# A two-layer encoder in one launch: 33 work slots instead of 30, a smaller ring for software DMAs, and the first MLP in stages of 6, 10 and 16 tiles

## The chip, the cores and the metric

The kernel runs on one core of a Trainium2 chip. Its time is the device time in microseconds (us), as a median of several runs; the profile is of one execution. Engines are TensorE (PE; its weight loads are PEld), VectorE (DVE), ScalarE (ACT), GpSimd (POOL) and SyncE (SP), which issues most DMAs.

## The reference, cut to what matters

The input is 512 tokens of 1024 values. Two pre-norm residual layers follow each other. Layer 0 has two attention groups side by side, layer 1 has 2-D neighbourhood attention, and each layer ends in a squared-ReLU MLP with 4096 hidden values:

```
def sq_relu_mlp(h, w_up, w_down):
    u = jax.nn.relu(h @ w_up)
    return (u * u) @ w_down
...
h = h + sq_relu_mlp(rmsnorm(h, norm_ffn[layer]), ffn_w_up[layer], ffn_w_down[layer])
...
q, k, v = jnp.split(h @ w_qkv, 3, axis=-1)
```

The first two lines of code are the MLP, the third its place in a layer, the last the start of layer 1's attention. All is float32.

## The kernel before, in words

**Number format.** Every float32 operand of a matmul is split into a high part, rounded to fp32r by an ACT copy, and a low part, the rest, by a VectorE subtraction. A product is three matmuls: high x high, high x low, low x high. Residual and activations lie transposed: hT has eight tiles of 128 features x 512 tokens.

**Slots.** Most intermediate results live in NSLOT = 30 tiles of 128 x 1024 (4 KB per partition each). A free list hands them out first in, first out (`take`, `give`); a new user waits until the last reader of the slot's former content is done. Weights as loaded lie in four further buffers (`raw`), the split weights in three pairs (`whi`, `wlo`).

**Two ways to multiply.** `product` (L445) and `product8` (L491) are plain: a tile of 128 outputs and 128 inputs costs three matmuls of 512 columns (`mm3`, L572). The class `Seven` (L338) takes two tiles of inputs, two of outputs and both halves of the tokens as a 2 x 2 block problem and does it in seven products of half the columns instead of eight: 21 matmuls of 256 columns (L418 to L420). For that it needs sums of the weight blocks, made on GpSimd by `seven_chunk` (L326 to L328), sums of the activations, made by `sums` (L360 to L366), and an addition of the seven results in `run` (L426 to L430). The split activations of such a product take 7 half slots for each pair of input tiles (`split`, L387 and L388).

**The MLP** (`mlp`, L1476). `SIZES[0] = (6, 10, 14, 2)` cuts the 32 tiles of U, the hidden values, into stages:

1. Six tiles of U by plain products, then their part of the down projection, also plain, over 4 + 4 output tiles. Beside it the input of the up projection is prepared for `Seven`.
2. Thirteen runs of `Seven`, two tiles of U each. `stage` (L1407) mixes ten tiles that come out split (`pair_evac`) with those that are kept raw (`raw_evac`): 14, and 2 more at the end.
3. The ten split tiles go through `product8`: eight output tiles at once in all eight banks, one row of weights after the other. Beside its matmuls, `convert` (L1469) turns the 14 raw tiles, as seven pairs, into the sums and splits that `Seven` wants, on VectorE and ACT, a step at a time; the steps keep the order of the program. `bias_rows` (L1441) runs beside it too and sends DMAs for layer 1 through SP's queue.
4. `Seven` over the seven pairs (u7), four groups of two output tiles (L1539 to L1546); each group ends in an evacuation that adds 1024 columns to two tiles of hT (L1543). In the first group `beside` splits the two last raw tiles.
5. `plain_last` (L1486): those two tiles in two plain products of four output tiles, evacuated by L1505.

Layer 1's MLP (`SIZES[1]`, `last_mlp`) has the same stages 1 to 4 and an end of its own.

**Weights.** Every product announces its chunks with `plan`; `weights(i)` splits two chunks ahead (`AHEAD`) and loads five ahead (`LOAD`). A chunk for `Seven` takes a slot when more than `reserve` slots are free, else a `raw` buffer (L322). `reserve` is 3 in the up stages, NSLOT (so never a slot) during stage 3, and 1 in stage 4.

**The start of layer 1** (L1557 to L1571). X, eight slots, holds hT times the norm's gain, split (L579, L580). `valuesC(0)` (L1625) multiplies X with 256 columns of weights in two chunks of four feature tiles: 32 groups of three matmuls (L1639 to L1641), the first 16 over feature tiles 0 to 3, the other 16 over tiles 4 to 7. `projC(0)` follows. When the third group has been issued, the sums of squares of hT are asked for (`sumsq_acc`, L587 and L589); after the 24th, `rows_r1` makes the row norms from them (L594, L602).

**Order.** Outside the opening and layer 1's attention (`fixed_order`) the framework orders the instructions of each engine by dependence and its own estimates; operations marked `held` keep the program's order.

**Software DMAs.** DMAs issued by GpSimd: eight small ones at the start (L144 to L151) and 32 in layer 1's attention that copy halves of K and Q (L1591, L1611, L1612). GpSimd also normalises the attention's weights (L1683). Their descriptors lie in a ring at the start of SBUF; `dynamic_dma_scratch_size` is its size per partition, 16384 bytes if it is not given.

Of the kernel before, what the change touches and what calls it, by code (L numbers as in the profile page):

```python
# [20 lines left out]
FF = 4 * D  # L21
EPS = 1e-6
NEG = -1e30
NSLOT = 30
ROWS = 8
COLS = 64
C_ID, C_I1, C_I2, C_ROPE = 0, 128, 178, 182
# [8 lines left out]
def encoder_kernel(ctx: ExitStack, tc: tile.TileContext, ins, out, dbg=None):  # L36
    nc = tc.nc
# [10 lines left out]

    free = list(range(NSLOT))

# [67 lines left out]
    def keep(shape, dt, name):  # L118
        return big.tile(shape, dt, tag=name, name=name)
# [127 lines left out]
    def rows(w, k0, nk):  # L247
        return w[k0 * P : (k0 + nk) * P, :].rearrange("(k p) n -> p k n", p=P)
# [5 lines left out]
    def plan(*spec, make=None):  # L254
        asked.append((make or chunk, spec))
        return len(asked) - 1
# [188 lines left out]
    def product(w, k0, xk, cols, evac, banks=None, kstep=2, stride=None, eng=None, order=None, nk=None):  # L445

        nk = nk or len(xk)
        runs = []  # L450
        for c, m in cols:
            if runs and runs[-1][1] + runs[-1][2] == c:
                runs[-1][2] += m
            else:
                runs.append([sum(r[2] for r in runs), c, m])
        ncols = sum(m for _, m in cols)
        offs = [sum(m for _, m in cols[:j]) for j in range(len(cols))]
        ids = []
        for kk in range(0, nk, kstep):
            n = min(kstep, nk - kk)  # L460
            if len(runs) > 1 and stride:
                src = w[(k0 + kk) * P : (k0 + kk + n) * P, :].rearrange("(k p) (z m) -> p k z m", p=P, m=stride)
                parts = [(0, ncols, src[:, :, 0 : len(runs), runs[0][1] : runs[0][1] + runs[0][2]])]
            else:
                src = rows(w, k0[kk // 2] if isinstance(k0, list) else k0 + kk, n)
                parts = [(o, m, src[:, :, c : c + m]) for o, c, m in runs]
            ids.append(plan(parts, n, ncols, None, eng))

        def run():
            bk = (banks or group)(len(cols))  # L470

            def one(kk, k, j):
                hi, lo = weights(ids[kk // kstep])
                x, o, m = xk[kk + k], offs[j], cols[j][1]
                mm3(bk[j][0:m, :], hi[:, k, o : o + m], lo[:, k, o : o + m], x[:, 0, :], x[:, 1, :],
                    kk + k == 0, kk + k == nk - 1)

            for kk in range(0, nk, kstep):
                n = min(kstep, nk - kk)
                last = kk + kstep >= nk  # L480
                for a in range(len(cols) if last else n):
                    for b in range(n if last else len(cols)):
                        one(kk, *((b, order[a] if order else a) if last else (a, b)))
                        yield MM3
                    if last:
                        j = order[a] if order else a
                        evac(j, bk[j][0 : cols[j][1], :])

        return run()
# [46 lines left out]
    def tiles(c0, n):  # L536
        return [(c0 + o, min(P, n - o)) for o in range(0, n, P)]
# [34 lines left out]
    def mm3(o, wh, wl, xh, xl, first, last):  # L572
        PE.matmul(o, wh, xh, start=first, stop=False)  # L573
        PE.matmul(o, wh, xl, start=False, stop=False)  # L574
        PE.matmul(o, wl, xh, start=False, stop=last)  # L575
# [727 lines left out]

    SIZES = (6, 10, 14, 2), (6, 10, 12, 4)

    def first_product(l):

# [8 lines left out]
        rb = keep([P, S], F32, "rb")  # L1318
        state = dict(c=SIZES[l][0], ids=None, plain=False, split=iter(()), late=iter(()))
        x7 = Seven(KD)  # L1320
# [155 lines left out]
    def mlp(l, last=None):  # L1476

        stage, ahead, later = first_product(l)
        reserve[0] = 3
        w = ins["ffn_w_down"][l]
        up4, gens4 = [], []

        def plain_last(k0, V):  # L1486
            left = list(V)
            gens4.extend(product(w, k0, up4, tiles(512 * c, 512), lambda j, b, c=c: ev(4 * c + j, b), nk=2 * len(V))
                         for c in range(2))

            def beside(m, i):
                if m == 0 and i % 8 == 4 and left:
                    w_ = left.pop(0)
                    for z in range(2):
                        U4.append(Slot())
                        up4.append(U4[-1].pair())
                        split(w_.t[:, S * z : S * z + S], up4[-1])
                    w_.free()

            return beside  # L1500

        U4 = []

        def ev(m, b):
            return DVE.tensor_tensor(hT[:, m, :], hT[:, m, :], b, op=ALU.add)  # L1505

        U, _, _, (at_u, _), _ = stage(SIZES[l][0])
        up = [s_.pair() for s_ in U]
        gens = [product(w, at_u, up, tiles(512 * c, 512), lambda j, b, c=c: ev(4 * c + j, b)) for c in range(2)]
        ahead()  # L1510
        for c, gen in enumerate(gens):
            for i, _ in enumerate(gen):
                later(c, i)
        for s_ in U:
            s_.free()
        U, R, V, (at_u, at_r), late = stage(*SIZES[l][1:])
        first = [k + z for k in at_u for z in range(2)]
        gen = product8(w, first, U, ev)
        u7 = Seven(2 * len(R))
        ids = [u7.plan(w, 256 * m, at_r) for m in range(4)]  # L1520
        k0 = 32 - 2 * len(V)
        beside = (last or plain_last)(k0, V)
        bias = iter(()) if last else bias_rows()
        reserve[0] = NSLOT
        work, at = convert(u7, R), 0
        for i, _ in enumerate(gen):
            if i in (1, 4, 6):
                next(late, None)
            next(bias, None)

            at += 9 * len(R) + 2
            while at > 0:
                next(work, None)
                at -= 8 * len(U) - 2
        for x in (work, bias):
            for _ in x:
                pass
        reserve[0] = 1
        for m in range(4):  # L1539

            def evac(w_):
                h2 = hT[:, 2 * m : 2 * m + 2, :]
                DVE.tensor_tensor(h2, h2, w_.t.rearrange("p (z n) -> p z n", z=2), op=ALU.add)  # L1543

            for i, _ in enumerate(u7.run(ids[m], evac)):
                beside(m, i)  # L1546
        u7.free()
        for gen in gens4:
            for _ in gen:
                pass  # L1550
        for s_ in U4:
            s_.free()
# [72 lines left out]
    def valuesC(g, banks):  # L1625

        ids = [plan([(0, 256, rows(w_qkv, kk, 4)[:, :, 2 * D + 256 * g : 2 * D + 256 * g + 256])], 4, 256)
               for kk in (0, 4)]

        def run():  # L1630
            bk = banks()
            VC[g] = []

            def one(c, k, i):
                hi, lo = (w[:, k, :] for w in weights(ids[c]))
                o = bk[i // 2][:, 256 * (i % 2) : 256 * (i % 2) + 256]
                x = XP[4 * c + k][:, :, i * P : (i + 1) * P]
                first = c == 0 and k == 0 and i % 2 == 0
                PE.matmul(o, x[:, 0], hi, start=first, stop=False, skip_group_check=True)  # L1639
                PE.matmul(o, x[:, 0], lo, start=False, stop=False, skip_group_check=True)  # L1640
                PE.matmul(o, x[:, 1], hi, start=False, stop=c == 1 and k == 3, skip_group_check=True)  # L1641

            for k in range(4):
                for i in range(4):
                    one(0, k, i)
                    yield 0.355
            for i in range(4):
                for k in range(4):
                    one(1, k, i)
                    yield 0.355  # L1650
                if i % 2:
                    VC[g].append(Slot())
                    v = VC[g][-1].t.rearrange("p (i h e) -> p i h e", i=2, h=4)
                    for ii in range(2):
                        src = bk[i // 2][:, 256 * ii : 256 * ii + 256].rearrange("p (h e) -> p h e", h=4)
                        r = hold["r1"][:, i - 1 + ii : i + ii]
                        ACT.activation(v[:, ii, :, 0:64], src, AF.Copy, scale=r)
                        soon(lambda v=v, ii=ii, src=src, r=r: DVE.scalar_tensor_tensor(
                            v[:, ii, :, 64:128], src, r, f32(v[:, ii, :, 0:64]), op0=ALU.mult, op1=ALU.subtract))

        return run()


# [376 lines left out]
```

## Time and profile before

| What | us |
|---|---|
| median of 3 runs | 1159.39 (1158.99 to 1159.63) |
| span of the profiled execution | 1157.2 |
| TensorE busy | 1146.8 |
| VectorE busy | 903.0 |
| ACT busy | 652.1 |
| GpSimd busy | 577.5 |
| thirteen up runs of layer 0 | 321.7 to 450.0 |
| its product8 | 450.0 to 505.2 |
| its seven-product groups (u7) | 505.2 to 574.7 |
| its last plain pair | 574.7 to 585.8 |
| first values of layer 1 | 585.8 to 597.1 |

The span runs from the first to the last instruction of the profiled execution, for which no other time is given; the runs' times also hold what lies around it. In the lines below, a row of the stretches gives start:end and length, then for each engine its busy time and, in brackets, its instructions; then the granted share of TensorE's clock, the share of the DMA engines, and GB/s. A row of a group gives line, engine, operation, output<-inputs, shapes and count, then the busy time, the mean ns of one, the idle time before them and what ended it. A row of the timeline gives start, duration, engine, line and operation.

### The profile page before, as it was taken

How to read it: one execution, taken by the hardware profiler on the slowest of the kernel's cores; microseconds unless marked ns; L12 is line 12 of the kernel's file. 1: busy time of each engine (PE TensorE's matmuls, PEld its weight loads, DVE VectorE, ACT ScalarE, POOL GpSimd, SP SyncE). 2: the span in 40 equal slices, each digit the busy share in tenths (PEclk: the TensorE clock that was granted, in tenths of full speed). 3: DMA queues.
4: the chain of work that ended last, by engine and by line, in shares of the span. 5: the costliest groups of instructions: out<-in, count | busy, mean ns of one | idle time of the engine just before them, and what ended most of it. 6: DMA issues, size and time to landing. Idle time of an engine off the chain costs nothing.

```text
span 1157.2 us, 20288 instructions
## 1 busy us (share of the span) xinstructions
PE 1146.8 (99%) x7276; PEld 1021.1 (88%) x7276; DVE 903.0 (78%) x1542; ACT 652.1 (56%) x1115; POOL 577.5 (50%) x708
## 2 busy tenths in 40 slices
PE   9999999999999999999999999999999999999997
PEld 7787888888899999899988998988889999988996
DVE  7887988878978887877685666668987788778675
ACT  6676876755346667433454556555553666743345
POOL 4366252216798882379402232231379889316930
PEclk9999999999999999999999999999999999999999
DMA  8322415122432326523436664443333233432332
GB/s 241 100 74 70 101 51 142 55 67 98 126 93 74 92 83 202 185 92 117 125 98 164 150 174 128 117 109 117 100 120 108 79 89 92 136 102 80 98 106 73
DMA packets 112148, 128.05 MB, mean 111 GB/s; under 512 B 9411, under 2 KB 94576, under 8 KB 112048
## 3 DMA queue, kind: packets, MB, share of 16 engines
q1 hardware_dynamic: 109424, 120.09, 35.4%
q0 software_dynamic: 2304, 6.31, 2.3%
q8 instruction: 57, 0.93, 0.4%
q14 instruction: 43, 0.35, 0.1%
q10 hardware_dynamic: 320, 0.36, 0.1%
HBM read 104.32 MB, written 6.29 MB: 96 GB/s over the span
## 4 chain that ended last, share of the span: by engine, by line
PE 96%; DVE 2%; DMA 1%; issue 1%; ACT 0%; POOL 0%; DVEq 0%; POOLq 0%
PE mm L573 9%; PE mm L575 9%; PE mm L574 9%; PE mm L418 4%; PE mm L420 4%; PE mm L419 4%; PE s L1097 3%; PE t L418 3%; PE t L420 3%; PE t L419 3%; PE o L1085 3%; PE s L573 3%; PE s L574 3%; PE s L575 3%; PE s L418 2%; PE s L420 2%
## 5 line engine op out<-in xcount | busy, mean ns | idle before, releaser
L573 PE MATMUL mm<-a,whi 128*128 128x512 f32 x440 | 178.6, 407 | 0.2
L332 ACT ACTIVATE whi<-a 128x896 fp32r<-128x896 f32 x105 | 99.7, 951 | 132.5 <-POOL a L328 39.2
L574 PE MATMUL mm<-a,whi 128*128 128x512 f32 x440 | 173.5, 394 | 0.0
L575 PE MATMUL mm<-a,wlo 128*128 128x512 f32 x440 | 173.5, 395 | 0.0
L333 DVE TENSOR_TENSOR wlo<-a,whi 128x896 fp32r<-128x896 f32 x105 | 133.1, 1272 | 49.2 <-ACT whi L332 46.1
L223 DVE TENSOR_TENSOR wlo<-raw,whi 128x1024 fp32r<-128x1024 f32 (+4 forms) x113 | 131.1, 1164 | 39.0 <-ACT whi L233 38.4
L233 ACT ACTIVATE whi<-raw 128x1024 fp32r<-128x1024 f32 (+3 forms) x116 | 109.1, 942 | 68.4 <-PE s L574 24.0
L418 PE MATMUL mm<-a,whi 128*128 128x256 f32 x410 | 115.1, 281 | 0.0
L420 PE MATMUL mm<-a,wlo 128*128 128x256 f32 x410 | 114.7, 280 | 0.0
L419 PE MATMUL mm<-a,whi 128*128 128x256 f32 x410 | 114.7, 280 | 0.0
L328 POOL TENSOR_TENSOR a<-a 128x128 f32<-128x128 f32 x105 | 102.9, 980 | 8.2
L326 POOL TENSOR_TENSOR a<-a 128x128 f32<-128x128 f32 x105 | 75.8, 722 | 57.3 <-DMA a<-in_ffn_w_up_dram 37.1
L575 PEld LDWEIGHTS mm<-a,wlo 128*128 128x128 f32 x440 | 82.5, 188 | 18.9
L573 PEld LDWEIGHTS mm<-a,whi 128*128 128x128 f32 x440 | 82.7, 188 | 17.6 <-issue 0.6
L574 PEld LDWEIGHTS mm<-a,whi 128*128 128x128 f32 x440 | 82.9, 188 | 15.3 <-DVE a L930 0.2
L327 POOL TENSOR_TENSOR a<-a 128x256 f32<-128x256 f32 x105 | 90.6, 863 | 8.2
L333 DVE TENSOR_TENSOR wlo<-raw,whi 128x896 fp32r<-128x896 f32 x51 | 62.4, 1226 | 35.4 <-ACT whi L332 35.4
L1683 POOL TENSOR_SCALAR p<-p,ti 128x256 f32<-128x256 f32 x64 | 35.6, 567 | 104.7 <-DVE ti L1682 91.5
L1105 POOL TENSOR_SCALAR p<-p,ti 128x512 f32<-128x512 f32 x64 | 45.0, 705 | 85.7 <-DVE ti L1104 63.6
L418 PE MATMUL t<-a,whi 128*128 128x256 f32 x296 | 83.1, 281 | 0.0
L419 PE MATMUL t<-a,whi 128*128 128x256 f32 x296 | 82.8, 280 | 0.0
L420 PE MATMUL t<-a,wlo 128*128 128x256 f32 x296 | 82.8, 280 | 0.0
(427 smaller groups left out, 3492.9 us busy)
## 6 DMA issues: line engine op xcount, KB each, us to landing
a<-in_ffn_w_up_dram SPq DMA_DIRECT2D x78, 256.0 KB
raw<-in_ffn_w_down_dram SPq DMA_DIRECT2D x38, 512.0 KB
raw<-in_od_w_qkv_dram SPq DMA_DIRECT2D x64, 128.0 KB
a<-in_ffn_w_down_dram SPq DMA_DIRECT2D x27, 256.0 KB
raw<-in_ffn_w_up_dram SPq DMA_DIRECT2D x26, 256.0 KB
raw<-in_ffn_w_down_dram SPq DMA_DIRECT2D x25, 256.0 KB
raw<-in_ffn_w_up_dram SPq DMA_DIRECT2D x12, 512.0 KB
a<-a SPq DMA_DIRECT2D x18, 256.0 KB
```

The source lines that it names most:

```text
L223: z = lambda: (eng or DVE).tensor_tensor(to, src, f32(high), op=ALU.subtract)
L233: ACT.activation(hi[:, 0:m], raw[:, 0:m], AF.Copy)
L327: POOL.tensor_tensor(r[:, 4:6], r[:, 2:3].to_broadcast([P, 2, P]), r[:, 0:7:6], op=ALU.add)
L328: POOL.tensor_tensor(r[:, 7], r[:, 3], r[:, 5], op=ALU.subtract)
L332: ACT.activation(hi[:, 0:896], raw[:, 128:1024], AF.Copy)
L333: DVE.tensor_tensor(lo[:, 0:896], raw[:, 128:1024], f32(hi[:, 0:896]), op=ALU.subtract)
L418: PE.matmul(o, wh, x[:, 0], start=kp == 0 and n in (0, 1, 3, 5), stop=False, skip_group_check=True)
L419: PE.matmul(o, wh, x[:, 1], start=False, stop=False, skip_group_check=True)
L420: PE.matmul(o, wl, x[:, 0], start=False, stop=kp == self.np - 1, skip_group_check=True)
L573: PE.matmul(o, wh, xh, start=first, stop=False)
L574: PE.matmul(o, wh, xl, start=False, stop=False)
L575: PE.matmul(o, wl, xh, start=False, stop=last)
```

## The change

NSLOT goes from 30 to 33, and the ring for software DMAs from 16384 to 4096 bytes per partition; the difference is three slots of 4096 bytes. `SIZES[0]` becomes (6, 10, 16, 0): the two last tiles of U are kept raw like the 14 others and form an eighth pair of u7, `convert` has eight pairs, and `plain_last` has nothing to do. In `valuesC(0)`, the second 16 groups run feature tiles 4 and 5 over all four token blocks first, and then 6 and 7 block by block; the other values (`g` > 0) keep their order.

```diff
-NSLOT = 30
+NSLOT = 33
...
-    SIZES = (6, 10, 14, 2), (6, 10, 12, 4)
+    SIZES = (6, 10, 16, 0), (6, 10, 12, 4)
...
         def plain_last(k0, V):
             left = list(V)
+            if not V:
+                return lambda m, i: None
             gens4.extend(product(w, k0, up4, tiles(512 * c, 512), lambda j, b, c=c: ev(4 * c + j, b), nk=2 * len(V))
...
                 for i in range(4):
                     one(0, k, i)
                     yield 0.355
+            late = 2 if g == 0 else 0
+            for k in range(late):
+                for i in range(4):
+                    one(1, k, i)
+                    yield 0.355
             for i in range(4):
-                for k in range(4):
+                for k in range(late, 4):
                     one(1, k, i)
                     yield 0.355
...
-    nc = _bacc.Bacc("TRN2", target_bir_lowering=False, num_devices=1)
+    nc = _bacc.Bacc("TRN2", target_bir_lowering=False, num_devices=1, dynamic_dma_scratch_size=4096)
```

## The prediction

> **What bounds the kernel now.** I read the page's engine totals and the chain that ended last first, then the busy times of five stretches, then what TensorE waited for.
>
> ```profile
> span 1157.2 us, 20288 instructions
> ...
> PE 1146.8 (99%) x7276; PEld 1021.1 (88%) x7276; DVE 903.0 (78%) x1542; ACT 652.1 (56%) x1115; POOL 577.5 (50%) x708
> ...
> PE 96%; DVE 2%; DMA 1%; issue 1%; ACT 0%; POOL 0%; DVEq 0%; POOLq 0%
> ```
>
> TensorE is busy 1146.8 of 1157.2 us and the chain is TensorE for 96%. Whatever shortens the kernel must take matmuls away, or some of the 10.4 us in which TensorE has none.
>
> ```profile
> core 0: us, PE busy (x) PEld busy (x) DVE busy (x) ACT busy (x) POOL busy (x), PEclk, DMA share, GB/s
> 449.99:505.18 55.19, 55.19 (x243) 45.08 (x242) 46.62 (x70) 24.36 (x36) 17.84 (x23) 1.00 0.56 177
> 505.18:574.69 69.51, 69.51 (x589) 69.40 (x588) 48.50 (x48) 27.98 (x33) 53.02 (x62) 1.00 0.35 111
> 574.69:585.83 11.14, 11.14 (x51) 9.01 (x49) 10.70 (x16) 8.54 (x14) 0.00 (x0) 1.00 0.40 114
> 585.83:597.14 11.31, 11.31 (x98) 11.31 (x96) 11.13 (x16) 4.96 (x8) 0.00 (x0) 1.00 0.37 106
> 1149.60:1157.20 7.60, 0.04 (x1) 0.00 (x0) 2.62 (x8) 2.21 (x6) 0.00 (x0) 0.74 0.62 187
> ```
>
> The first four rows are consecutive stages of layer 0's down projection and the start of layer 1: the ten single rows of weights (product8), the seven-product pairs (x588), the last plain pair (48 matmuls), the first values of layer 1 (96). TensorE has no gap in any of them, at full clock. The last row is the end: 7.6 us without matmuls, which the change leaves alone.
>
> ```profile
> PE o L157 <- POOL zeros L130: 1.0, 1, 1.0
> PE t L602 <- DVE ti L190: 0.2, 1, 0.2
> PE t L594 <- DVE acc L630: 0.2, 1, 0.2
> PE t L594 <- DVE acc L589: 0.2, 1, 0.2
> PE t L602 <- DVE r L1566: 0.2, 1, 0.2
> ```
>
> So of the 10.4 us, 1.0 lie at the start and 7.6 at the end. About 1.8 us are left for waits in between, the shown ones among them. That is the most that any better ordering can win.
>
> **The change part by part.** *Matmuls.* Layer 0's last two U tiles leave the plain product and become an eighth seven-product pair. Which tiles the up stage makes, and in which order, stays the same: thirteen pairs, the last one kept raw in both. The plain stage goes: 2 products x 4 tiles x 2 rows x 3 = 48 matmuls of 512 columns, 11.14 us by its row (232 ns each). The eighth pair adds 4 groups x 7 products x 3 = 84 matmuls of 256 columns. The row of that stage gives 69.51/588 = 118.2 ns each, so 9.93 us. The difference is **-1.21 us**, all on the path, because TensorE is the path.
>
> By the Trainium skill, TensorE: Matmul & The Clock Gate, section Back-to-back issue gap, a stream of load-and-multiply pairs sustains about 131 ns at 512 columns and 81 at 128; that would price the 48 at 6.3 us and the 84 at 6.8 to 11.0, a loss of 0.5 to 4.7. The rows above have 232 and 118 ns in this stream, so the trace does not agree.
>
> *Loads and splits of the pairs' weights.* Away go two 512 KB chunks with an ACT copy and a VectorE subtraction each; four chunks of 256 KB come, each with three GpSimd sums.
>
> ```profile
> L328 POOL TENSOR_TENSOR a<-a 128x128 f32<-128x128 f32 x105 | 102.9, 980 | 8.2
> L326 POOL TENSOR_TENSOR a<-a 128x128 f32<-128x128 f32 x105 | 75.8, 722 | 57.3 <-DMA a<-in_ffn_w_up_dram 37.1
> L327 POOL TENSOR_TENSOR a<-a 128x256 f32<-128x256 f32 x105 | 90.6, 863 | 8.2
> ```
>
> A chunk costs GpSimd 0.98 + 0.72 + 0.86 = 2.57 us, and TensorE uses one in 21 x 118.2 = 2.48 us. GpSimd loses 0.09 us per chunk, 2.9 us over 32. It starts on them inside the previous stage (17.84 us of it there, seven chunks ahead), and 32 x 2.57 = 82 us fit into 69.5 + 9.9 + 17.8 = 97. I take 0; without that lead the cost is +2.9 us. The new spare slots let every such chunk have a slot instead of sharing the four raw buffers with other loads: nothing gained either, as TensorE has no gap to close there.
>
> *Converting the eighth pair* (its sums and splits on VectorE, during product8).
>
> ```profile
> L388 DVE TENSOR_TENSOR a<-a,a 128x512 fp32r<-128x512 f32 x14 | 10.7, 762 | 0.7 <-ACT a L387 0.5
> L388 DVE TENSOR_TENSOR a<-sc,a 128x512 fp32r<-128x512 f32 x7 | 5.3, 761 | 0.0
> L360 DVE TENSOR_TENSOR sc<-a 128x512 f32<-128x512 f32 x7 | 5.1, 722 | 0.0
> L388 DVE TENSOR_TENSOR a<-a,a 128x256 fp32r<-128x256 f32 x7 | 3.5, 493 | 0.0
> L392 DVE TENSOR_TENSOR a<-a 128x256 f32<-128x256 f32 x7 | 3.4, 485 | 0.2
> L363 DVE TENSOR_TENSOR a<-a,sc 128x256 f32<-128x256 f32 x7 | 3.4, 485 | 0.2
> ```
>
> Seven pairs now; one costs 2 x 0.762 + 0.761 + 0.722 + 0.493 + 2 x 0.485 = **4.47 us**. VectorE's idle time in this stage is 55.19 - 46.62 = 8.57 us, so it rises from 84% to 93%. What must not come late behind it stands in the next rows: VectorE's split of the tenth row and its first evacuation, and on TensorE the first readers of both.
>
> ```profile
> 493.68 1.45 DVE L223 TENSOR_TENSOR wlo<-raw,whi 128x1024 fp32r<-128x1024 f32 x1 [0.78 <-ACT whi L233]
> ...
> 500.24 0.67 DVE L1505 TENSOR_TENSOR hT<-hT,s 128x512 f32<-128x512 f32 x1
> ```
>
> ```profile
> 495.40 0.39 PE L575 MATMUL s<-p,wlo 128*128 128x512 f32 x1
> 505.18 0.28 PE L418 MATMUL s<-a,whi 128*128 128x256 f32 x1
> ```
>
> The split ends at 495.13 and is read at 495.40: 0.27 us to spare. The evacuation ends at 500.91 and its bank is wanted at 505.18: 4.27 us. If all added work goes into idle time nothing is late; if none does, the split is late by 4.47 - 0.27 = 4.2 us. I take **+0.1**, because the idle time is nearly twice the added work.
>
> *The joint with layer 1.* The plain stage was also a cover of 11.14 us between the last seven-product group and the values. Without it hT 6 and 7 are ready only behind that group's evacuation (L426 to L430, L1543).
>
> ```profile
> 574.54 0.68 DVE L427 TENSOR_TENSOR a<-a,mm 128x512 f32<-128x512 f32 x1
> ...
> 579.19 1.22 DVE L1543 TENSOR_TENSOR hT<-hT,a 128x1024 f32<-128x1024 f32 x1
> ...
> 582.45 0.75 DVE L580 SCALAR_TENSOR_TENSOR a<-hT,gT,a 128x512 fp32r<-128x512 f32 x1
> ```
>
> ```profile
> 578.11 0.72 ACT L579 ACTIVATE a<-hT,gT 128x512 fp32r<-128x512 f32 x1 [2.27 <-DVE hT L1505]
> ```
>
> The chain ends at 580.41, 5.7 us after the last matmul of the group at 574.69. Three L1505 additions of the plain product stand inside it (0.6 us apart each); they go, and 3.9 us are left. Then come two ACT halves (0.72 and some 0.62, as they pipeline) and the VectorE halves (0.75): X 6 is whole about 5.5 us and X 7 about 6.2 us after the group. The values take 11.31/32 = 0.353 us per group of three. In the old order X 6 is wanted after 16 + 2 groups, 6.4 us, and X 7 after 19, 6.7 us: on the edge. In the new order X 4 and 5 run for eight groups first, and X 6 is wanted at 24 groups, 8.5 us, X 7 at 8.8. The reordering buys 2 us of cover and no matmul. One edge remains: X takes eight slots, the free list holds five when the pairs' 28 are given back, and the fifth is the evacuation's own, free only after L1543. X 4 is then whole at about 3.9 + 0.7 + 0.8 = 5.4 us and is wanted at 5.7. Bounds: 0, and 1.2 us if one 128x1024 split lands in front. I take **+0.2**.
>
> *What gets earlier.* The squares of hT 0 to 5 no longer queue behind the plain product's additions (VectorE was busy 21.8 of 22.5 us in those two stretches), so the wait of L594 for acc should go.
>
> ```profile
> 597.84 0.39 PE L573 MATMUL mm<-a,whi 128*128 128x512 f32 x1
> 598.41 0.27 PE L594 MATMUL t<-ones,acc 128*128 128x1 f32 x1 [0.18 <-DVE acc L589]
> ```
>
> The next start comes 0.57 us after a matmul that takes 0.23: 0.34 us lost. I take **-0.3**. The wait of L602 for L1566 behind it is a chain of small operations that stays.
>
> *The smaller ring.* Only GpSimd's own DMAs use it.
>
> ```profile
> q0 software_dynamic: 2304, 6.31, 2.3%
> ...
> a<-a POOLq DMA_DIRECT2D x16, 256.0 KB, 3.7
> ```
>
> Each comes down in 3.7 us, in bursts of four per pair of heads. If the ring held one burst no longer, GpSimd would wait up to 3.7 us in eight places, 30 us, with the attention's normalisations queued behind; if it holds it, nothing changes, and nothing can be gained. I take 0: no wait for a ring shows on any of these now, and 2304 packets over 16 engines are 144 each for the whole run. By the Trainium skill, DMA: Bandwidth & Descriptors, section Terms, a descriptor has 16 bytes, so 4096 bytes would be 256 of them, an estimate by which the ring does not even wrap; no run here shows it.
>
> **Sum:** -1.21 + 0.1 + 0.2 - 0.3 = -1.2 us, against the profiled span 1157.2: 1156.0. The page gives no other time for that execution; the median of the runs is 1159.39, 2.2 us above the span, and I carry that over: **1158.2**. This is 0.10%, and about 0.2% (2.3 us) is what a measurement of this kernel can tell from no change.
>
> **The rivals.**
> - *More waits go (faster).* Other slots and another order around the joint also take the waits that stay in my sum. For it: they are short and hang on VectorE. Against: 1.8 us is all there is, 0.3 of it already counted. At most 1159.4 - 1.2 - 1.5 = 1156.7, or 1156.4 if the two small losses stay away too.
> - *The joint takes the gain back.* X 4 or X 6 late by 1 to 2 us: 1159 to 1160.4. For it: margins of 0.3 and 2 us. Against: VectorE loses 5.5 us of additions there.
> - *VectorE overflows in product8 (slower).* Place: the tenth row's split and the evacuations at 500 to 505 us. Price: 4.2 us at most, 1162.4. It ends slower than before once less than 3.0 of the 8.57 us of idle time can be filled, and slower by over 0.2% once less than 0.7 can. For it: a margin of 0.27 us, and ACT and VectorE alternate on the splits. Against: 5.5 us of that idle time are L223's waits for ACT, in which other splits can run.
> - *Small matmuls are not half price, or the change does nothing.* If a 256-column one cost what a 512-column one does, 84 x 232 ns - 11.1 = +8.4, 1167.8. If the ring's size frees no usable slot or binds, the time is 1159.4 or far above. The rows of 118 ns and of 144 packets speak against both.
>
> **How the numbers follow.** Forecast 0.52 (1157.4 to 1159.0), more waits go 0.20, the joint 0.12, VectorE 0.12, the last 0.04. The range 1156.6 to 1161.0 leaves out a quarter of the faster case, most of VectorE's upper part and the last. Faster by over 0.2% (under 1157.07): 0.16 of the faster rival and 0.03 of the forecast, 0.19. Slower (over 1161.71): 0.07 of VectorE's, 0.01 of the joint, 0.03 of the last, 0.11. Within: 0.70.
>
> **What would show it.** 672 seven-product matmuls in about 79.4 us, directly followed by L1639; no plain stage; the wait of L594 for acc gone; VectorE near 51 us in product8; L1683 on GpSimd with no new wait. Wrong would be: a wait of TensorE for L223 or L1505 around 495 to 510 us, a gap among the values at L1639 to L1641, GpSimd's sums (L328) named by ACT with TensorE behind it, or a change outside layer 0's end and layer 1's start, where only the slots differ and I count nothing.

## The result: slower by 0.45%, and the profile after

| | before | after |
|---|---|---|
| median of four runs each, same chip | 1159.34 us (1158.99 to 1159.63) | 1164.41 us (1164.29 to 1164.54) |
| ratio, 95% interval | | 1.0045 (1.003 to 1.0059) |
| span of the profiled execution | 1157.2 us | 1162.6 us |

The forecast was 1158.2 us, its range ended at 1161.0. The changed kernel is 5.1 us slower than before. (In after, lines from L1488 on stand 2 and from L1655 on 7 lines lower than in before: L1545 is before's L1543.)

The page's engine totals and the chain that ended last, of after:

```profile
span 1162.6 us, 20364 instructions
...
PE 1148.2 (99%) x7312; PEld 1023.3 (88%) x7312; DVE 911.4 (78%) x1541; ACT 655.7 (56%) x1119; POOL 585.8 (50%) x720
...
PE 89%; POOL 4%; DVE 3%; issue 1%; ACT 1%; DVEq 0%; POOLq 0%; ACTq 0%
```

TensorE's share of the chain fell from 96% to 89%, and GpSimd, which had 0%, now has 4% of it. TensorE's own 99% hardly shows this: the time in which it counts as idle grew from 10.4 to 14.4 us, and part of its waits counts as busy (80.33 us in u7 below, where e3, a run below without waits in u7, has 79.10 for the same matmuls). The stretches of layer 0's product8 and u7 in after, and of everything from there to layer 1's MLP:

```profile
core 0: us, PE busy (x) PEld busy (x) DVE busy (x) ACT busy (x) POOL busy (x), PEclk, DMA share, GB/s
451.40:506.72 55.32, 55.32 (x242) 45.04 (x241) 51.22 (x74) 25.57 (x38) 21.48 (x26) 1.00 0.54 171
506.72:590.11 83.39, 80.33 (x673) 79.41 (x672) 61.96 (x63) 37.98 (x48) 60.30 (x70) 1.00 0.32 98
590.11:885.39 295.28, 294.18 (x1658) 254.00 (x1657) 214.13 (x469) 152.75 (x320) 97.24 (x147) 1.00 0.48 136
```

Product8 is as forecast: VectorE 51.22 us busy, no wait of TensorE. The plain stage is gone. But the 672 seven-product matmuls, forecast at 79.4 us, took **83.39**. What TensorE waited for, longest first:

```profile
PE mm L420 <- DVE wlo L333: 1.9, 2, 1.3
PE o L157 <- POOL zeros L130: 1.0, 1, 1.0
PE s L420 <- DVE wlo L333: 0.7, 1, 0.7
PE o L1641 <- ACT a L579: 0.5, 1, 0.5
PE mm L418 <- ACT whi L332: 0.5, 1, 0.5
```

Three of the five are the splits (L332, L333) of the pairs' weights, a wait that before didn't have at all. The wait of L1641 belongs to the joint with layer 1 and comes up again at the end. Two rows of the timeline of GpSimd, in the beginning of u7, show where it starts; the bracket is the idle time ahead of an instruction and what ended it:

```profile
509.73 0.46 POOL L328 TENSOR_TENSOR a<-a 128x128 f32<-128x128 f32 x1
520.92 0.63 POOL L326 TENSOR_TENSOR a<-a 128x128 f32<-128x128 f32 x1 [10.73 <-DMA a<-in_ffn_w_down_dram]
```

GpSimd stands still for 10.73 us and then works to the end with one more pause of 1.0 us. The stretch from there to its last sum:

```profile
520.92:583.15 62.23, 60.27 (x508) 59.76 (x507) 46.68 (x46) 26.66 (x34) 57.72 (x66) 1.00 0.28 86
```

66 sums are 22 chunks, 62.23 / 22 = **2.83 us** each, where TensorE uses one in 2.48. Ten chunks were done before the pause. In the timelines, the sums of the tenth end 18.8 us ahead of its first matmul, those of the eleventh, the first after the pause, 8.5 us, and those of the 22nd 3.6 us. So the lead goes down by a pause at once and then, beside the second pause, by some 0.35 us a chunk. At the 23rd TensorE waits for the first time, and there the order of the chunks counts too. Two rows of GpSimd and one of ACT:

```profile
557.87 0.46 POOL L328 TENSOR_TENSOR a<-a 128x128 f32<-128x128 f32 x1
...
559.64 0.46 POOL L328 TENSOR_TENSOR a<-a 128x128 f32<-128x128 f32 x1
```
```profile
560.14 1.79 ACT L332 ACTIVATE whi<-a 128x896 fp32r<-128x896 f32 x2 [4.17 <-POOL a L328]
```

The sums of GpSimd's 23rd chunk were done at 558.33, yet ACT stood idle until those of its 24th were done at 560.10, and then copied two chunks at once: GpSimd did these two in the other order than TensorE uses them. The same happens in the last group at 583.16. There, too, a split at 579.80 started 1.2 us after its copy was done, as VectorE was with work for layer 1 (L589, L580). Before has the same change of order at 534.20 (ACT idle for 3.25 us) and no wait of TensorE, so it is the short lead that makes such delays count. How much of u7's loss is theirs was not taken apart.

By stages of the spans, from the stretches of each kernel (us):

| | start | 13 up runs | product8 | u7 + plain pair | values to layer 1's MLP | that MLP | end |
|---|---|---|---|---|---|---|---|
| before | 321.70 | 128.29 | 55.19 | 80.65 | 294.35 | 269.19 | 7.8 |
| after | 322.62 | 128.78 | 55.32 | 83.39 | 295.28 | 268.80 | 8.4 |
| slots and ring alone (e1) | 322.81 | 128.45 | 55.33 | 80.33 | 294.59 | 269.69 | 8.6 |
| ring alone (e2) | 322.19 | 128.29 | 55.15 | 80.63 | 294.34 | 269.20 | 7.8 |
| reserve 3 (e3) | 322.71 | 128.48 | 55.30 | 79.10 | 294.83 | 268.73 | 8.4 |
| reserve 3, old order (f2) | 322.52 | 128.78 | 55.30 | 79.09 | 294.68 | 268.39 | 7.8 |
| reserve 3, slots local (g1) | 321.72 | 128.29 | 55.14 | 79.18 | 294.23 | 269.08 | 7.8 |

Of the 5.4 us between the spans of before and after, u7 has 2.7, and the rest is small shares in the start, the up runs, the values and the end.

### The profile page after: what moved, and what is told of

Its sections match the earlier page's. It is cut to its first block, busy times and chain, and to the rows that moved or that the text cites. A ratio compares the mean times of both kernels' runs of the same rounds, so it can differ in the third digit from the quotient of the medians.

```text
span 1162.6 us, 20364 instructions
## 1 busy us (share of the span) xinstructions
PE 1148.2 (99%) x7312; PEld 1023.3 (88%) x7312; DVE 911.4 (78%) x1541; ACT 655.7 (56%) x1119; POOL 585.8 (50%) x720
## 4 chain that ended last, share of the span: by engine, by line
PE 89%; POOL 4%; DVE 3%; issue 1%; ACT 1%; DVEq 0%; POOLq 0%; ACTq 0%
PE mm L573 9%; PE mm L575 8%; PE mm L574 8%; PE mm L420 3%; PE mm L419 3%; PE mm L418 3%; PE s L1097 3%; PE t L420 3%; PE t L419 3%; PE t L418 3%; PE o L1085 3%; PE s L574 2%; PE s L573 2%; PE s L575 2%; PE t L1072 2%; PE s L420 2%
## 5 line engine op out<-in xcount | busy, mean ns | idle before, releaser
L333 DVE TENSOR_TENSOR wlo<-a,whi 128x896 fp32r<-128x896 f32 x148 | 187.4, 1272 | 78.4 <-ACT whi L332 78.0
L332 ACT ACTIVATE whi<-a 128x896 fp32r<-128x896 f32 x148 | 140.2, 950 | 157.8 <-PE o L419 39.7
L573 PE MATMUL mm<-a,whi 128*128 128x512 f32 x434 | 176.3, 407 | 0.2
L326 POOL TENSOR_TENSOR a<-a 128x128 f32<-128x128 f32 x148 | 105.3, 711 | 137.5 <-DMA a<-in_ffn_w_up_dram 76.6
L574 PE MATMUL mm<-a,whi 128*128 128x512 f32 x434 | 171.2, 394 | 0.0
L223 DVE TENSOR_TENSOR wlo<-raw,whi 128x1024 fp32r<-128x1024 f32 (+4 forms) x111 | 130.5, 1180 | 34.7 <-ACT whi L233 34.1
L327 POOL TENSOR_TENSOR a<-a 128x256 f32<-128x256 f32 x148 | 140.0, 946 | 11.5
L233 ACT ACTIVATE whi<-raw 128x1024 fp32r<-128x1024 f32 (+3 forms) x114 | 106.7, 939 | 69.1 <-PE s L574 27.4
L328 POOL TENSOR_TENSOR a<-a 128x128 f32<-128x128 f32 x148 | 130.1, 879 | 11.6
L420 PE MATMUL mm<-a,wlo 128*128 128x256 f32 x420 | 117.9, 281 | 1.9 <-DVE wlo L333 1.9
L418 PE MATMUL mm<-a,whi 128*128 128x256 f32 x420 | 117.8, 281 | 0.5 <-ACT whi L332 0.5
L419 PE MATMUL mm<-a,whi 128*128 128x256 f32 x420 | 117.5, 280 | 0.0
L575 PEld LDWEIGHTS mm<-a,wlo 128*128 128x128 f32 x434 | 81.4, 188 | 18.6
L418 PE MATMUL t<-a,whi 128*128 128x256 f32 x304 | 85.2, 280 | 0.0
L419 PE MATMUL t<-a,whi 128*128 128x256 f32 x304 | 85.1, 280 | 0.0
L420 PEld LDWEIGHTS mm<-a,wlo 128*128 128x128 f32 x420 | 79.0, 188 | 2.4 <-DVE wlo L333 2.3
```

The source lines that it names most:

```text
L223: z = lambda: (eng or DVE).tensor_tensor(to, src, f32(high), op=ALU.subtract)
L233: ACT.activation(hi[:, 0:m], raw[:, 0:m], AF.Copy)
L327: POOL.tensor_tensor(r[:, 4:6], r[:, 2:3].to_broadcast([P, 2, P]), r[:, 0:7:6], op=ALU.add)
L328: POOL.tensor_tensor(r[:, 7], r[:, 3], r[:, 5], op=ALU.subtract)
L332: ACT.activation(hi[:, 0:896], raw[:, 128:1024], AF.Copy)
L333: DVE.tensor_tensor(lo[:, 0:896], raw[:, 128:1024], f32(hi[:, 0:896]), op=ALU.subtract)
```

## The experiments

Three theories were set against each other for u7 and for the rest; the expectations call them A, B and D. **A:** layer 1's first loads, which in SP's queue stand ahead of the pairs' loads, bring those late. **B:** the number of buffers that chunks can lie in caps how far GpSimd gets ahead, and as it is slower than TensorE it never makes that good. **D:** the three slots shift the work of other stages too. Medians stand beside those of before on the same chip.

### The parts alone

**e1_slots** (before, with the slots and the ring of after):

```diff
-NSLOT = 30
+NSLOT = 33
...
-    nc = _bacc.Bacc("TRN2", target_bir_lowering=False, num_devices=1)
+    nc = _bacc.Bacc("TRN2", target_bir_lowering=False, num_devices=1, dynamic_dma_scratch_size=4096)
```

> The kernel before with 33 slots and the small ring alone; stages and order of the values as before. Theory A (the loads of the pairs' weights come late: layer 1's loads were put ahead of 22 of them in SP's queue, GpSimd sat idle 10.7 us and TensorE paid 4.0 us in the seven-product stage): the seven pairs' loads are not overtaken here, so that stage stays at 69.5 us without a wait; what is left is the drift of the changed kernel outside the MLP's end (0.9 us before the up projection, 0.5 in the up runs, 0.9 in layer 1's attention), 1161 to 1162. Theory B (the slots themselves do it: every chunk goes through few slots and GpSimd's lead is lost whatever the order): this stage waits 1 us or more, 1163 or above. Theory C (the drift comes from the ring): the same 1161 to 1162, but then the run with the small ring alone has it too.

1161.12 us against 1159.09, ratio 1.0015 (1.0006 to 1.0024). The slots alone cost some 2 us, none of it in u7, but mostly in the start, layer 1's MLP and the end. B as first put (the slots themselves make u7 wait, 1163 or above) did not come true. GpSimd had the same pause in u7, here put down to the split that gives a buffer back, yet no wait of TensorE followed:

```profile
521.10 0.46 POOL L326 TENSOR_TENSOR a<-a 128x128 f32<-128x128 f32 x1 [10.87 <-DVE wlo L333]
```

With 28 chunks instead of 32 the stage ends before the lead is used up: 3.6 us of it were left at the last chunk. So B became a matter of lead and rate.

**e2_ring** (before, with the second half of that diff alone):

> The kernel before with the small ring alone. If the ring does nothing: 1159.3, and no new wait on GpSimd. Theory C (GpSimd's DMAs wait for ring space or move slower): 1160 to 1162, GpSimd's DMAs in layer 1's attention over 3.7 us to landing or a gap ahead of them.

1159.07 against 1159.09, ratio 1.0 (0.9991 to 1.0009), and no stage moved by more than 0.5 us. The ring's size does nothing.

### The order of SP's queue, or the buffers

SP's queue in after, where the pause of GpSimd begins and ends:

```profile
505.15 0.37 SPq L324 DMA_DIRECT2D a<-in_ffn_w_down_dram  x1
508.54 3.16 SPq L211 DMA_DIRECT2D raw<-in_od_w_qkv_dram  x2
512.34 3.95 SPq L214 DMA_DIRECT2D raw<-in_od_w_qkv_dram  x8
516.39 0.41 SPq L324 DMA_DIRECT2D a<-in_ffn_w_down_dram  x1
```

Ten loads for layer 1 stand between two chunks: theory A. But VectorE's row says something else too:

```profile
515.18 1.09 DVE L333 TENSOR_TENSOR wlo<-a,whi 128x896 fp32r<-128x896 f32 x1 [1.31 <-ACT whi L332]
```

This split ends at 516.27, 0.12 us ahead of the load at 516.39. It is the split of the sixth chunk, and the load is that of the eleventh: theory B, with five buffers.

**f1_pin** (after, with layer 1's loads behind the pairs' loads in SP's queue, by the program's order):

```diff
+    def load(dst, src):
+        i = SP.dma_start(dst, src)
+        if pin[0]:
+            tc.keep_in_program_order(i)
...
-                SP.dma_start(dst, src)
+                load(dst, src)
...
+        pin[0] = l == 0
```

> The changed kernel, all chunks of the eight pairs in slots, but layer 1's ten loads kept behind the pairs' loads in SP's queue. Theory A (the place of these loads in the queue made GpSimd idle 10.7 us): that idle time goes, the seven-product stage takes 79 to 79.6 us, total 4 us under the changed kernel, 1159.8 to 1160.6. Rival B (five slots are too few for a chunk every 2.5 us, whoever is first in the queue): GpSimd still idles several us and the stage keeps 1 us of waits or more, above 1161.

1164.59 against 1159.39, ratio 1.0046 (1.0033 to 1.0059); u7 83.24 us. Lines stand 7 lower here. The loads for layer 1 are gone from between the chunks, and the pause is still there, in the first row. The second is a wait of SP's queue, with its sum, how many times, and the longest:

```profile
519.90 0.46 POOL L333 TENSOR_TENSOR a<-a 128x128 f32<-128x128 f32 x1 [9.70 <-DMA a<-in_ffn_w_down_dram]
```
```profile
SPq L331 <- DVE wlo L340: 47.5, 17, 11.0
```

SP had nothing else in its queue and waited 11.0 us for a split to give a buffer back. **Theory A falls.**

**e3_reserve3** (after, in which a chunk takes a slot only when more than three are free, so that the four raw buffers are used as well):

```diff
-        reserve[0] = 1
+        reserve[0] = 3
```

> The changed kernel with reserve 3 instead of 1 in the seven-product stage: every other chunk goes into the raw buffers again, which keeps layer 1's loads behind the pairs' in SP's queue. Theory A: the waits of TensorE for L333 and L332 (4.0 us) are gone, the stage takes 672 x 118.2 ns = 79.4 us, total 1159.5 to 1160.5. Rival (GpSimd is just too slow for 32 chunks, 2.8 us each against 2.48 us of TensorE): 2 us or more of those waits stay, 1162 to 1163.

1159.84 against 1159.09, ratio 1.0007 (0.9998 to 1.0016): 4.3 us of after's 5.1 are gone by one number. u7 has no wait. The rows are the stretch of u7, then GpSimd's first sum after its pause, then the stretch from that sum to its last:

```profile
506.49:585.59 79.10, 79.10 (x674) 79.09 (x672) 64.34 (x63) 37.99 (x48) 62.26 (x70) 1.00 0.34 106
```
```profile
510.79 1.34 POOL L326 TENSOR_TENSOR raw<-raw 128x128 f32<-128x128 f32 x1 [4.06 <-DMA raw<-in_ffn_w_down_dram]
```
```profile
510.79:576.42 65.63, 65.63 (x560) 65.63 (x560) 51.85 (x49) 30.48 (x38) 62.02 (x69) 1.00 0.34 106
```

The pause is 4.06 us instead of 10.73. In the last row GpSimd does 69 sums, 23 chunks, in 65.63 us: 2.85 us a chunk, no faster than in after. It starts on them with a lead of 14.5 us instead of 8.5, and 6.7 are left at the last chunk. The matmuls give the forecast gain: 79.10 for 80.65 us, -1.55.

### How many buffers

**f4_31_raw** (after with 31 slots and a ring of 12288, and all chunks of stage 4 in the four raw buffers), **g3_raw5** and **g4_raw6** (the same with five and six raw buffers and the ring of 4096):

```diff
-NSLOT = 33
+NSLOT = 31
...
-        reserve[0] = 1
+        reserve[0] = NSLOT
```

```diff
-        raw = slot.t if slot else wp.tile([P, 1024], F32, tag="raw", bufs=4, name=nm("raw"))
+        raw = slot.t if slot else wp.tile([P, 1024], F32, tag="raw", bufs=6, name=nm("raw"))
```

> 31 slots, and no chunk of the seven-product stage takes a slot: all through the four raw buffers. If the wait for a slot that an evacuation holds made the 3 us of waits with 31 slots: they go, the stage takes 79.1 to 79.6 us, total 1159 to 1160. Rival (four buffers are too few, or GpSimd too slow): 2 us or more of waits for L332 or L333, 1161 to 1163.

> 31 slots, all chunks of stage 4 through raw buffers as in the run with four (u7 84.47 us there), but with five of them. Theory B (the number of buffers that chunks can take decides): u7 at 80.5 to 83.0 us, GpSimd's idle time down from 16.7 us to 10 to 14. Rival (waits come from raw buffers being shared with layer 1's loads, or from 31 slots): u7 84 to 85.

> As the run before, with six raw buffers. Theory B: u7 at 79.0 to 80.0 us without a wait for L333, GpSimd's idle time under 9 us. Rival: 84 to 85 as with four. The whole time is open, since the plain loads of the other stages can run further ahead too: 1157.5 to 1161 by B.

1165.55 against 1159.39, ratio 1.0054 (1.0041 to 1.0068); 1163.44 against 1159.07, 1.0035 (1.0021 to 1.0048); 1162.64 against 1159.07, 1.0029 (1.002 to 1.0038). The stretches from the first sum after the pause to the last one, of f4 and of g4:

```profile
510.29:584.73 74.44, 71.07 (x596) 70.25 (x595) 54.16 (x54) 32.63 (x41) 70.20 (x81) 1.00 0.33 104
```
```profile
510.33:581.55 71.22, 70.46 (x597) 70.05 (x596) 56.03 (x54) 32.66 (x41) 67.29 (x75) 1.00 0.37 116
```

In both the pause ends at 510.3 us, when the first split of u7 has given a buffer back and a load has come into it; e3's ended at 510.79. What differs is how many chunks are left: 81 sums are 27, 75 are 25. The table puts the runs together. Buffers are counted from the timelines: by how many chunks a load is behind the split at whose end it is issued.

| run | buffers | chunks left after the pause | lead of the first of them, us | us per chunk | u7, us |
|---|---|---|---|---|---|
| f4 | 4 | 27 of 32 | 4.7 | 2.76 | 84.47 |
| after | 5, later 4 | 22 of 32 | 8.5 | 2.83 | 83.39 |
| g3 | 5 | 26 of 32 | 7.2 | 2.80 | 82.85 |
| g4 | 6 | 25 of 32 | 9.6 | 2.85 | 81.20 |
| e3 | 8 | 23 of 32 | 14.5 | 2.85 | 79.10 |
| before | 7, at times 6 | 20 of 28 | 12.1 | 2.73 | 69.51 |

A buffer is worth 2.4 to 2.5 us of lead, one chunk of TensorE, and between four and six of them 1.6 us of u7. After starts with more lead than g3 and yet has a longer u7; there the changed order of its last chunks adds to it. In f4, g3 and g4 no copy of ACT shows such a change, and TensorE waits all the same, so the buffers act without it. The expectation for four was exceeded (1165.55, where even the rival had at most 1163), that for five was met (82.85 in 80.5 to 83.0), and that for six was missed (81.20 instead of 79 to 80): the direction of B is right, but six are not enough for 32 chunks. The rival, that four to six raw buffers give the same, falls.

**e5_31slots** (after with 31 slots and a ring of 12288 alone; chunks have the raw buffers and now and then a slot):

> The changed kernel with 31 slots and a ring of 12288 bytes: two slots fewer, so the pairs' chunks share the raw buffers as before. Theory A: no wait in the seven-product stage, 79.4 us, and less of the drift elsewhere, 1158.2 to 1160. Rival of GpSimd's rate: the 4 us stay, 1162 or above.

1162.74 against 1159.09, ratio 1.0027 (1.0016 to 1.0038); u7 82.08 us. A's 79.4 did not come, the rival's 1162 or above did. What SP waited for there includes this:

```profile
SPq L324 <- DVE hT L1545: 11.1, 3, 6.9
```

Six to seven buffers by the count, but one is the slot of the group's evacuation, and its chunk came up to 6.9 us late. So the count alone doesn't price this run.

**h2_before_raw** (before, with all 28 chunks of stage 4 in the four raw buffers; neither slots nor the eighth pair):

```diff
-        reserve[0] = 1
+        reserve[0] = NSLOT
```

> The kernel before with one change: in stage 4 no chunk takes a slot, so that all 28 go through the four raw buffers. Theory B (the count of buffers, not the eighth pair nor the three slots, makes the waits): the first 28 chunks of the 31-slot run with raw buffers alone took 73.0 us, so u7 rises from 69.5 to 72.5 to 73.5 with waits for L333, 1161.8 to 1163.2. Rival (seven pairs have lead enough with any buffers, or the eighth pair makes the waits): u7 69 to 70, 1158.8 to 1160.

1161.83 against 1159.35, ratio 1.0022 (1.0013 to 1.0031). Before, too, now waits for its splits:

```profile
PE mm L420 <- DVE wlo L333: 1.0, 1, 1.0
```

u7 is 70.61 us, 1.1 more than in before; 2.0 were expected as the least. The mechanism is there without the eighth pair, smaller than thought, since GpSimd took only 2.67 us a chunk in this run. Another 2.2 us lie in layer 1's MLP (271.42 for 269.19). Its pairs go through the same line, but so do those of f4 and g3, which have 269.27 and 268.78 there; so this part stays open.

### GpSimd's rate

**g2_sum_dve** (after, with the first of the three sums on VectorE in stage 4) and **h1_two_sums** (after, with that sum left out in stage 4 and a load in its place):

```diff
-        POOL.tensor_tensor(r[:, 6], r[:, 0], r[:, 1], op=ALU.subtract)
+        (DVE if reserve[0] == 1 else POOL).tensor_tensor(r[:, 6], r[:, 0], r[:, 1], op=ALU.subtract)
```

```diff
+        if reserve[0] == 1:
+            SP.dma_start(r[:, 6], rows(w, k0, 2)[:, 0, c0 : c0 + P])
+        else:
             POOL.tensor_tensor(r[:, 6], r[:, 0], r[:, 1], op=ALU.subtract)
```

> The kernel after with one change: in stage 4 the first of the three sums of a chunk (L326) runs on VectorE, so that GpSimd needs about 1.9 us a chunk instead of 2.8. Theory B (too few buffers let GpSimd idle, and at 2.8 us a chunk against TensorE's 2.5 it can't make the loss good): GpSimd still idles about 10 us around 510 to 520, but u7 comes to 79.4 to 80.2 us without waits for L333 in its last group; 1160.2 to 1161.2. Rival (a late load or split, not GpSimd's rate, holds TensorE up): u7 stays at 83 to 84 us, 1164 to 1165.

> The kernel after, but in stage 4 of both MLPs the first sum of a chunk (L326) is left out, and a 64 KB load fills its place, so that the result is another: GpSimd then has two sums, about 1.8 to 2.1 us a chunk against TensorE's 2.5, and VectorE gets nothing new. Theory B as it stands now (the buffers set how far GpSimd is ahead when stage 4 starts, and its rate of 2.8 us a chunk, slower than TensorE, eats that lead): u7 at 79.2 to 80.2 us without waits in its last group, 1160.0 to 1161.3. Rival (a closed loop: with four to five buffers a load waits for a split and the split for the load, whatever GpSimd's rate): u7 at 82 to 85, 1163 to 1165.5.

g2: 1165.45 against 1159.07, ratio 1.0053 (1.004 to 1.0065), u7 84.93 us. A miss. What VectorE and GpSimd waited for between 480 and 600 us:

```profile
DVE a L326 <- DMA a<-in_ffn_w_down_dram: 12.9, 9, 3.7
```
```profile
POOL a L327 <- DVE a L326: 22.7, 10, 13.6
```

VectorE stood 12.9 us before sums whose chunk hadn't come, with the splits that free the buffers behind them. This run made a new wait and says nothing of GpSimd's rate. It was therefore taken away without touching VectorE: h1 gave 1159.15 against 1159.35, ratio 0.9995 (0.9986 to 1.0004). Lines stand 3 lower here:

```profile
507.36:586.45 79.09, 79.09 (x673) 79.09 (x672) 60.81 (x62) 38.19 (x48) 43.25 (x46) 1.00 0.38 119
```
```profile
POOL a L330 <- DMA a<-in_ffn_w_down_dram: 22.9, 9, 13.3
```

GpSimd's longest pause is 13.3 us, longer than in after, and u7 has no wait at all; u7 and the total are even a little under what B had forecast. The rival, a closed loop whatever the rate, falls. So the pause does harm only because GpSimd is slower than TensorE behind it: with two sums a chunk it catches up. **B holds in both its halves**, the buffers (e3, f4, g3, g4) and the rate (h1).

### The reordered values, and slots where they are needed

**f2_r3_old_order** (e3 with the old order of the first values):

```diff
-            late = 2 if g == 0 else 0
+            late = 0
```

> Reserve 3 as in the run before, and the old order of the first values. If the reordering covers what the plain stage covered: TensorE waits 0.5 to 2 us among the values for X 6 and 7, total 1160.4 to 1162. Rival (that chain is in time anyway): the same as with the new order, 1159.8.

1159.13 against 1159.39, ratio 0.9999 (0.999 to 1.0008); values and attention 294.68 us, 294.83 with the new order (e3). The reordering buys nothing that shows. TensorE waits 0.2 us for X in both, after 16 groups, where X 4 is wanted in either order.

**f3_local3** (e3 with the three slots in use only from product8 to the end of u7 in layer 0) and **g1_local_back** (the same, but the three that came free last are taken out, not the first in the list):

```diff
-    free = list(range(NSLOT))
+    free = list(range(30))
...
+        if l == 0:
+            give(30, 31, 32)
...
         u7.free()
+        if l == 0:
+            take(3)
```

```diff
-            take(3)
+            del free[-3:]
```

> Reserve 3, and the three new slots are in the free list only from layer 0's product8 to the end of its seven-product stage; elsewhere 30 as before. Theory D (the 33 slots cost 2 us elsewhere, as the run with the slots alone has it, through another order of the schedule): these 2 us go, 1158.0 to 1158.5, 0.6 to 1.1 under the kernel before. Rival (the 2 us come from the eighth pair's stage or from the placement in memory): 1159.5 to 1160.2.

> The kernel after with a reserve of 3 in stage 4 and the three new slots in use from product8 to the last pair of layer 0 only; then the three slots that came free last are taken out of the list, so that X finds spare ones. Theory B and D (the 33 slots cost some 2 us in other stages, and the buffers of the chunks 4 us in u7): 672 matmuls in 79.1 to 79.6 us, no wait of L1645 in the values (13.0 to 13.5 us, then layer 1 up to its MLP about 281.9), layer 1's MLP and tail as before; 1157.9 to 1158.9, some 0.5 to 1.2 us under the kernel before. Rival (what the slots cost elsewhere is not the slots but any new order): 1159.5 to 1160.5.

f3: 1162.67 against 1159.39, ratio 1.0029 (1.0018 to 1.0039). u7 is fine with 79.60 us, but now the values wait:

```profile
PE o L1645 <- ACT a L579: 2.4, 1, 2.4
```

The first three in the list were the spare ones, so a tile of X got the evacuation's slot, free only after that group's last addition. The values up to layer 1's MLP took 298.52 us. With the last three taken out, g1 gave **1157.64** against 1159.07, ratio 0.9987 (0.9978 to 0.9995), the fastest of all. Its longest waits and its u7:

```profile
PE o L157 <- POOL zeros L130: 1.0, 1, 1.0
PE t L602 <- DVE ti L190: 0.2, 1, 0.2
PE t L594 <- DVE acc L630: 0.2, 1, 0.2
PE o L1085 <- DVE a L1075: 0.2, 1, 0.2
```
```profile
505.15:584.33 79.18, 79.18 (x674) 79.13 (x672) 63.95 (x63) 37.99 (x48) 62.22 (x71) 1.00 0.34 106
```

The start, the up runs and the end are as in before (321.72, 128.29 and 7.8 us). This bears D out for the sum, of 1 to 2 us; why the slots cost what they do in each stage was not taken apart, and single executions blur it. f2, with all slots everywhere, has 7.8 us at the end and 268.39 in layer 1's MLP, no more than before. And f3, with 30 slots in the list until product8, has 322.78 us at the start, where it waited 1.3 us for the load of x.

## Why the prediction was wrong, point by point

- **Loads and splits of the pairs' weights: the step that failed.** It took 0 and said of the slots "nothing gained either", with +2.9 us as the cost without the lead. It summed GpSimd's time (82 us into 97) as if GpSimd could work ahead without limit. But GpSimd is held up until a buffer is free. Giving every chunk a slot took the four raw buffers out of use: the seven buffers of before became five, at times four. That made a pause of 10.73 us. And the loss per chunk was 0.35 us instead of 0.09, since a chunk took 2.83 us: the 2.57 were a mean over 105 chunks of the whole kernel, and in before's own u7 a chunk took 2.73 (54.52 us for the last 20). u7 lost 4.3 us by it (83.39 against 79.10 with reserve 3), the short lead and what it lets through taken together.
- **The slots elsewhere: counted as nothing, cost 1 to 2 us.** e1 shows them alone (+2.0), g1 without them is back at before's stages. With the 4.3 us of u7, e1's 2.0 make up the 6.2 us between 1158.2 and 1164.41.
- **Matmuls: right.** Forecast -1.21; e3 shows -1.55 and g1 -1.47 for u7 and the plain pair.
- **Product8: right.** VectorE near 51 us, in fact 51.22, and no wait. That +0.13 us were measured for +0.1 forecast is luck: e1 has 55.33 us without an eighth pair, and g1 has 55.14 with it.
- **The joint: right in size, where u7 is not disturbed.** +0.2 and -0.3 were forecast, -0.1 together; f2 and e3 have +0.3 and +0.5, g1 -0.1. The wait of L594 for acc L589 is gone from the list. The one edge that the prediction named is real: TensorE waits for X 4 after 16 groups, 0.5 us in after (the wait of L1641 for L579), 0.2 in e3 and f2, and f3 has the same kind of wait at an earlier tile, 2.4 us. The evacuation's chain took 5.4 us in after, not 3.9; a 128x1024 split of 1.22 us (L223) stands in it, the case that the prediction had as its upper bound. That the reordering buys 2 us of cover stays an argument: f2 did as well without it.
- **The ring: right.** Nothing.
- **The rivals.** None of them named the buffers. The one that ends slower put it on VectorE's overflow in product8, which did not come. The list of what would be wrong did hold it: GpSimd's sums named by ACT with TensorE behind them, a gap among the values, and a change outside the joint. All three came.

## What to carry to other kernels

A helper engine that is a little slower than the main one can be covered only by work done ahead, and buffers cap that lead: count how many chunks fit between a load and the split that frees its place, multiply by the main engine's time for one, take off what the load and the sums take (5.2 to 5.3 us in f4, g3, g4, e3 and before), and set what is left against the loss per chunk times the chunks that are left. A rule like "take a slot when one is free" can reduce the buffers in use when more slots are added, because the other pool falls idle. Give new buffers only to the stage that wants them, and when they are taken back, take those that come free last.

## What the runs showed of the hardware that was not expected

GpSimd's sums of 128x128 mostly take either 0.46 or 1.2 to 1.3 us. Two rows of VectorE and two of GpSimd in after's u7:

```profile
546.15 0.68 DVE L427 TENSOR_TENSOR a<-a,mm 128x512 f32<-128x512 f32 x1
...
554.59 1.34 DVE L333 TENSOR_TENSOR wlo<-a,whi 128x896 fp32r<-128x896 f32 x1
```
```profile
546.52 0.46 POOL L326 TENSOR_TENSOR a<-a 128x128 f32<-128x128 f32 x1
...
554.95 1.31 POOL L326 TENSOR_TENSOR a<-a 128x128 f32<-128x128 f32 x1
```

The slow one starts while VectorE is in a split (L333, 554.59 to 555.93) and ends 0.33 us after it; the fast one starts in the middle of an addition that reads a PSUM tile (mm). In u7 of after, of the 21 sums by L326 and L328 that began at least 0.3 us before the end of such a split 19 took over 1.0 us, of the 26 others 3. With all of VectorE's instructions that have two inputs in SBUF (L580, L589 and L1545 beside L333), it is 22 of 28, and of the 19 others none. The Trainium skill, SBUF — State Buffer, section Who interferes with whom, says that a VectorE instruction with two inputs in SBUF contends with a GpSimd instruction that reads SBUF, that the port pair they share is an exclusive lock, and that the order of issue decides who blocks. This trace agrees: L333 has two such inputs, L427 one. So each chunk's own split slows the sums of a later chunk by up to 0.85 us each. Undisturbed, the three sums of a chunk took 1.8 us (558.29 to 560.10), less than TensorE's 2.48; the mean of 2.57 that the prediction used then holds what VectorE did beside them. No run here took the splits away to show it by itself.
